# The normalised input of a two-layer trunk, 128 bytes further back in SBUF

## The chip, the cores and the metric

The kernel runs on one core of one Trainium2 chip. Its metric is the time of one execution on the device in microseconds, taken as the median of several; smaller is better.

## The reference, cut to what matters

Two layers, each made of an FFN, a token mixer and a second FFN. All three read a normalised and modulated input u, and add their gated result to the residual x (256 positions by 1024 channels). Everything is float32.

```python
for l in range(DEPTH):                       # 2
    mod = c_act @ w_ada[l] + b_ada[l]
    sh1, sc1, g1, sh2, sc2, g2, sh3, sc3, g3 = jnp.split(mod, 9, axis=-1)
    x = x + 0.5 * g1 * swiglu(modulate(x, sh1, sc1), ffn1_gate[l], ffn1_up[l], ffn1_down[l])
    x = x + g2 * token_mix(modulate(x, sh2, sc2), ..., w_in[l], ...)
    x = x + 0.5 * g3 * swiglu(modulate(x, sh3, sc3), ffn2_gate[l], ffn2_up[l], ffn2_down[l])
return rms_norm(x) * final_norm

def swiglu(u, w_gate, w_up, w_down):         # 1024 -> 2816 -> 1024
    return (jax.nn.silu(u @ w_gate) * (u @ w_up)) @ w_down
```

The token mixer projects u by w_in (1024 to 4024 columns), runs sparse attention and latent attention on the parts, merges them by sigmoid gates and projects the result by w_out.

## The kernel before

**Three matmuls for one.** Each product is made of float32r operands that are split in two parts: hi is the value rounded by ScalarE (L177 for weights, L336 for the input), lo is what is left, by VectorE (L182, L337). A product is hi x hi + hi x lo + lo x hi, so every tile of 128 x 128 takes three matmuls, all issued by the helper at L103. The weight's parts are whi and wlo, the input's uhi and ulo, the FFN's hidden layer's hh and hl.

**Which operand streams.** There are two forms. In `ws_tile` (L430) a weight tile of 128 columns is stationary and the input streams, 256 columns: the loop over groups of the gate and up projections (L606 to L622) and some parts of the token mixer (L701, L722, L881). In `xs_group` (L372) the input or the hidden layer is stationary and the weight streams, 512 columns (in the token mixer also 408, 288 and 256): the first 512 columns of gate and up, the merge gates, the down and the output projections. Each matmul loads its own stationary operand, also where it is the same as before.

**The order of the work.** Weights come by SP's DMA queue into four raw buffers. Scheduling within an engine follows the program's order, with a few exceptions that the change does not touch. Between the groups of an FFN the modulation of the next sub-layers is computed: VectorE sums the products (`ada_half`, L225), and TensorE then sums over partitions (the tiles `tr<-acc,ones` in the trace).

**Places in SBUF.** A pool lays its tiles one behind the other, in the order of their first use, and the pools lie one behind the other. The place of each tile in its partition follows from the sizes in front of it. In bytes, modulo 512 (the two halves of 128 positions and the eight channel blocks of the input are 512 and 1024 bytes apart, so the numbers hold for all of them):

| tiles | pool | modulo 512 |
|---|---|---|
| raw; whi and wlo (four in `wsp`, three in `fu`) | raws, wsp, fu | 96 |
| hh and hl (an FFN's hidden layer), cT (the latents), oa, ob, yt | ffn, tm | 96 |
| yk (half of the merged branches) | tm | 192 |
| x, uhi, ulo | keep | 288 |
| acc, g, and the scratch tiles xn, uf, rtmp | keep, scr | 288 |

The pool `keep` begins at 96. Its first tile is `apart` (L121), 48 floats or 192 bytes, that nothing reads; then come x (L123), uhi and ulo (L359, L360), then acc and g. `new_u` is called once for each sub-layer and hands out the same buffers each time.

Of the kernel before, what the change touches and what calls it, by code (L numbers as in the profile page):

```python
# [10 lines left out]
F32 = mybir.dt.float32  # L11
# [5 lines left out]
P = 128  # L17
# [60 lines left out]
def hybrid_trunk(ctx, tc, t, out):  # L78
    nc = tc.nc
# [7 lines left out]
    keep = ctx.enter_context(tc.tile_pool(name="keep", bufs=1))  # L87
# [30 lines left out]
    nc.gpsimd.memset(binit, 0.0)  # L118
    cact = const.tile([P, KD], F32, name="cact")
    nc.scalar.activation(cact, c_in, AF.Silu)  # L120
    apart = keep.tile([P, 48], F32, name="apart")  # L121
    nc.gpsimd.memset(apart, 0.0)
    x = keep.tile([P, NH, D], F32, name="x")  # L123
    colmask = tab[:, TAB_COL:TAB_COL + 32]
# [227 lines left out]
    def flush(ps):  # L352
        for p in list(ps):
            if p in pending:
                pending.remove(p)
                p[1]()

    def new_u():
        uhi = keep.tile([P, KD, S], F32R, name="uhi", tag="uhi")  # L359
        ulo = keep.tile([P, KD, S], F32R, name="ulo", tag="ulo")  # L360
        return uhi, ulo


# [743 lines left out]
    def start_norm(l, sub):  # L1107
        u = new_u()

        def post(hf):  # L1110
            pending.append([DELAY[hf], norm_mod(hf, u[0], u[1], mods[l, 3 * sub + 1], mods[l, 3 * sub])])
        return u, post
# [15 lines left out]
    fnorm = [None, None]  # L1128
    subs = [(l, sub) for l in range(DEPTH) for sub in range(3)]
    nxt = new_u()  # L1130
    xn = []
    for hf in range(NH):
# [60 lines left out]
```

## Time and profile before

| | |
|---|---|
| median of 3 runs | 1196.02 us (1194.01 to 1196.26) |
| the profiled execution | 1195.32 us |
| its span, from the first to the last instruction | 1193.5 us |
| TensorE busy, weight loads | 1156.5 us (97%), 1016.1 us (85%) |
| VectorE, ScalarE, POOL busy | 946.5, 640.8, 19.4 us |
| mean granted TensorE clock | 0.994 |

The ends of matmuls are modelled, so the time of one matmul in a row is not the pace: the pace is the distance between the starts of two that follow each other, or the length of an unbroken piece over its count. Several groups of the page are the same work for the three products.

### The profile page before, as it was taken

The numbers are of one execution on the slowest core, as the hardware profiler recorded it, in microseconds if no ns is written. First come the engines' busy times: TensorE is split into PE (matmuls) and PEld (weight loads), VectorE is DVE, ScalarE is ACT, GpSimd is POOL, SyncE is SP. The second block draws the span as 40 slices with busy tenths as digits, with TensorE's granted clock in tenths as the row PEclk, the third lists the DMA queues.
The fourth block names the chain that finished last, engine by engine and source line by source line (L and its number), as shares of the span: only waits on it lengthen the run. The fifth ranks groups of instructions, "written<-read, shape, count | busy, mean of one in ns | idle before, by whom it ended". The sixth has DMA issues, their size and how long they took to land.

```text
span 1193.5 us, 20212 instructions
## 1 busy us (share of the span) xinstructions
PE 1156.5 (97%) x7886; PEld 1016.1 (85%) x7886; DVE 946.5 (79%) x1885; ACT 640.8 (54%) x1152; POOL 19.4 (2%) x19
## 2 busy tenths in 40 slices
PE   5999999999999999999999999998999999999997
PEld 3799988799977789998879999787997778999985
DVE  4899998878888898798579889865878888865553
ACT  4444544557676565444455444454677756554441
POOL 0000000100000000000000000001000000000000
PEclk9999999899999999999999999999999999999999
DMA  9989999586623579989739979954664253985540
GB/s 330 318 292 327 343 344 326 200 237 197 177 74 107 177 231 306 308 290 321 271 106 317 319 261 364 342 191 139 181 194 118 78 188 131 298 260 201 173 146 36
DMA packets 201970, 274.95 MB, mean 230 GB/s; under 512 B 13613, under 2 KB 119815, under 8 KB 201875
## 3 DMA queue, kind: packets, MB, share of 16 engines
q1 hardware_dynamic: 201119, 273.02, 69.9%
q8 instruction: 62, 1.02, 0.3%
q10 hardware_dynamic: 756, 0.64, 0.2%
q14 instruction: 33, 0.27, 0.1%
HBM read 272.60 MB, written 1.05 MB: 229 GB/s over the span
## 4 chain that ended last, share of the span: by engine, by line
PE 87%; DVE 7%; DMA 2%; issue 2%; ACT 1%; SPq 1%; DVEq 0%; ACTq 0%
PE mm L103 78%; PE tr L106 3%; DVE wlo L182 3%; PE sc L103 2%; PE po L103 2%; DMA raw<-in_w_ada 2%; PE tr L103 2%; DVE win L710 1%; ACT whi L177 0%; DVE rs L305 0%; DVE rtmp L439 0%; DVE x L440 0%; DMA c_in<-in_c 0%; DVE kd L732 0%; DVE acc L528 0%
## 5 line engine op out<-in xcount | busy, mean ns | idle before, releaser
L182 DVE TENSOR_TENSOR wlo<-raw,whi 128x1024 fp32r<-128x1024 f32 (+5 forms) x400 | 428.0, 1085 | 122.6 <-ACT whi L177 121.4
L177 ACT ACTIVATE whi<-raw 128x1024 fp32r<-128x1024 f32 (+5 forms) x400 | 364.0, 935 | 235.6 <-PE mm L103 102.3
L103 PE MATMUL mm<-uhi,whi 128*128 128x256 f32 x1248 | 348.7, 279 | 0.0
L103 PE MATMUL mm<-uhi,wlo 128*128 128x256 f32 x1248 | 347.3, 278 | 0.0
L103 PE MATMUL mm<-ulo,whi 128*128 128x256 f32 x1248 | 347.3, 278 | 0.0
L103 PEld LDWEIGHTS mm<-ulo,whi 128*128 128x128 f32 x1248 | 236.4, 189 | 0.5
L103 PEld LDWEIGHTS mm<-uhi,whi 128*128 128x128 f32 x1248 | 234.3, 188 | 2.5 <-issue 1.8
L103 PEld LDWEIGHTS mm<-uhi,wlo 128*128 128x128 f32 x1248 | 234.4, 188 | 0.0
L225 DVE SCALAR_TENSOR_TENSOR acc<-raw,cact,acc 128x512 f32<-128x512 f32 x224 | 167.4, 749 | 6.3 <-DMA raw<-in_w_ada 3.4
L103 PE MATMUL mm<-whi,hh 128*128 128x512 f32 x352 | 138.3, 393 | 0.0
L103 PE MATMUL mm<-whi,hl 128*128 128x512 f32 x352 | 137.1, 390 | 0.0
L103 PE MATMUL mm<-wlo,hh 128*128 128x512 f32 x352 | 137.0, 389 | 0.0
L103 PE MATMUL mm<-wlo,uhi 128*128 128x512 f32 (+3 forms) x336 | 126.5, 377 | 3.7 <-DVE wlo L182 3.7
L103 PE MATMUL mm<-whi,uhi 128*128 128x512 f32 (+3 forms) x336 | 127.2, 381 | 2.6 <-ACT uhi L541 2.6
L103 PE MATMUL mm<-whi,ulo 128*128 128x512 f32 (+3 forms) x336 | 127.4, 380 | 1.7 <-DVE ulo L337 1.7
L482 ACT ACTIVATE hh<-hf 128x256 fp32r<-128x256 f32 x70 | 29.1, 416 | 95.7 <-DVE hf L481 95.7
L103 PEld LDWEIGHTS mm<-whi,hh 128*128 128x128 f32 x352 | 66.1, 188 | 15.1 <-issue 1.8
L103 PEld LDWEIGHTS mm<-whi,hl 128*128 128x128 f32 x352 | 66.1, 188 | 13.9
L103 PEld LDWEIGHTS mm<-wlo,hh 128*128 128x128 f32 x352 | 66.1, 188 | 13.4
L103 PEld LDWEIGHTS mm<-wlo,uhi 128*128 128x128 f32 x336 | 64.3, 191 | 14.1 <-DVE wlo L182 4.6
L103 PEld LDWEIGHTS mm<-whi,uhi 128*128 128x128 f32 x336 | 63.9, 191 | 13.7 <-ACT uhi L541 3.0
L103 PEld LDWEIGHTS mm<-whi,ulo 128*128 128x128 f32 x336 | 64.3, 191 | 12.5 <-DVE ulo L337 3.6
(243 smaller groups left out, 1347.5 us busy)
## 6 DMA issues: line engine op xcount, KB each, us to landing
raw<-in_w_ada SPq DMA_DIRECT2D x72, 1024.0 KB, 7.9
raw<-in_ffn_gate SPq DMA_DIRECT2D x41, 1024.0 KB, 7.5
raw<-in_ffn_up SPq DMA_DIRECT2D x41, 1024.0 KB, 6.2
raw<-in_ffn_down SPq DMA_DIRECT2D x40, 1024.0 KB, 7.4
raw<-in_w_in SPq DMA_DIRECT2D x18, 1024.0 KB, 6.5
raw<-in_w_in SPq DMA_DIRECT2D x16, 512.0 KB, 6.4
raw<-in_w_out SPq DMA_DIRECT2D x8, 1024.0 KB, 5.1
raw<-in_ffn_down SPq DMA_DIRECT2D x8, 512.0 KB
```

Source lines behind the costliest of these rows:

```text
L103: nc.tensor.matmul(o, a, b, start=start, stop=stop)
L106: nc.tensor.transpose(o, a, ident)
L177: nc.scalar.activation(a, s, AF.Copy)
L182: nc.vector.tensor_tensor(b, s, a.bitcast(F32), ALU.subtract)
L225: nc.vector.scalar_tensor_tensor(acc, rv[:, jj, :], cj, binit if j + jj == 0 else acc, ALU.mult, ALU.add)
L482: nc.scalar.activation(h[0][:, f, :], hf32, AF.Copy)
L710: nc.vector.tensor_tensor(win[i][jj * 64:(jj + 1) * 64, 8 * a:8 * a + 8, g, :], pv[g * 64:(g + 1) * 64, jj, :, a:a + 15], cols[0][jj * 64: ...
```

## The change

`apart` shrinks from 192 to 64 bytes, so x, uhi and ulo move back by 128 bytes, to 160 modulo 512. A new tile of 128 bytes, `behind`, is taken behind ulo, when `new_u` is called first, so acc, g and all later pools stay where they are. Nothing reads `behind`; it is set to zero once.

```diff
-    apart = keep.tile([P, 48], F32, name="apart")
+    apart = keep.tile([P, 16], F32, name="apart")
     nc.gpsimd.memset(apart, 0.0)
     x = keep.tile([P, NH, D], F32, name="x")
...
+    behind = []
+
     def new_u():
         uhi = keep.tile([P, KD, S], F32R, name="uhi", tag="uhi")
         ulo = keep.tile([P, KD, S], F32R, name="ulo", tag="ulo")
+        if not behind:
+            behind.append(keep.tile([P, 32], F32, name="behind"))
+            nc.gpsimd.memset(behind[0], 0.0)
         return uhi, ulo
```

With it the input lies 64 bytes past the place of the weights' parts, modulo 512, where it lay 192 past it. The order of instructions on TensorE, VectorE, ScalarE and SyncE stays as it was. On POOL one instruction comes in. Before, at the start of the program (apart, pad and binit are the tiles set to zero there, hid is one of the token mixer):

```order
L118 MEMSET binit 128x512
masks.py:199 ISA
masks.py:199 AFFINE_SELECT ident<-ident 128x128
L122 MEMSET apart 128x48
L129 MEMSET pad 128x80
L766 MEMSET hid 128x32
```

And now:

```order
L118 MEMSET binit 128x512
masks.py:199 ISA
masks.py:199 AFFINE_SELECT ident<-ident 128x128
L122 MEMSET apart 128x16
L129 MEMSET pad 128x80
L365 MEMSET behind 128x32
L771 MEMSET hid 128x32
```

One memset got shorter, and one of 32 floats a partition stands behind that of pad.

## Rows read from the trace of the kernel before

**Rows 1.** The page's busy times: us (share of the span) x instructions
```profile
PE 1156.5 (97%) x7886; PEld 1016.1 (85%) x7886; DVE 946.5 (79%) x1885; ACT 640.8 (54%) x1152; POOL 19.4 (2%) x19
```

**Rows 2.** The page's chain that ended last, by engine and line
```profile
PE 87%; DVE 7%; DMA 2%; issue 2%; ACT 1%; SPq 1%; DVEq 0%; ACTq 0%
PE mm L103 78%; PE tr L106 3%; DVE wlo L182 3%; PE sc L103 2%; PE po L103 2%; DMA raw<-in_w_ada 2%; PE tr L103 2%; DVE win L710 1%; ACT whi L177 0%; DVE rs L305 0%; DVE rtmp L439 0%; DVE x L440 0%; DMA c_in<-in_c 0%; DVE kd L732 0%; DVE acc L528 0%
```

**Rows 3.** The page's costliest groups: count | busy us, mean ns | idle before
```profile
L103 PE MATMUL mm<-uhi,whi 128*128 128x256 f32 x1248 | 348.7, 279 | 0.0
```

**Rows 4.** The chain in order of time: start us, length us, what
```profile
67.52 20.38 PE mm L103 x173
89.14 11.31 PE mm L103 x96
100.92 10.89 PE mm L103 x96
...
479.01 22.61 PE mm L103 x192
...
715.99 21.97 PE mm L103 x192
...
1057.94 127.72 PE mm L103 x840
```

**Rows 5.** Stretches, matmuls that read ulo: PE busy (count), clock, DMA share, GB/s
```profile
67.50:87.60 20.10, 15.98 (x58) 1.00 0.98 332
...
100.90:111.60 10.70, 8.72 (x32) 1.00 0.99 337
844.20:855.40 11.20, 8.96 (x33) 1.00 0.50 161
```

**Rows 6.** Weight loads from 480 to 500 us, then from 526 to 546
```profile
L103 PEld LDWEIGHTS mm<-ulo,whi 128*128 128x128 f32 x57 | 10.9, 192 | 0.0
...
L103 PEld LDWEIGHTS mm<-ulo,whi 128*128 128x128 f32 x59 | 11.1, 188 | 0.0
```

**Rows 7.** TensorE in order of time, cT streaming: start us, length us
```profile
293.85 0.40 PE L103 MATMUL mm<-cT,whi 128*128 128x256 f32 x2
...
294.93 0.28 PE L103 MATMUL mm<-cT,whi 128*128 128x256 f32 x1
```

**Rows 8.** The same, weights streaming in 256 columns, input stationary
```profile
277.77 0.28 PE L103 MATMUL mm<-whi,ulo 128*128 128x256 f32 x1
...
279.78 0.28 PE L103 MATMUL mm<-wlo,uhi 128*128 128x256 f32 x1
```

**Rows 9.** The same, 512 columns, hidden layer stationary
```profile
574.73 0.39 PE L103 MATMUL mm<-whi,hl 128*128 128x512 f32 x1
...
576.77 0.39 PE L103 MATMUL mm<-whi,hl 128*128 128x512 f32 x1
```

**Rows 10.** The same, 512 columns, input stationary
```profile
239.75 0.39 PE L103 MATMUL mm<-whi,uhi 128*128 128x512 f32 x1
...
241.81 0.39 PE L103 MATMUL mm<-whi,uhi 128*128 128x512 f32 x1
```

**Rows 11.** The same, 512 columns, yk stationary, and what follows it
```profile
405.90 2.97 PE L103 MATMUL mm<-us,yk 128*128 128x512 f32 x12
408.71 0.40 PE L103 MATMUL mm<-whi,yt 128*128 128x512 f32 x1
```

**Rows 12.** Groups by form: the 512-column matmuls with the input stationary
```profile
L103 PE MATMUL mm<-whi,ulo 128*128 128x512 f32 x240 | 97.8, 408 | 1.7 <-DVE ulo L337 1.7
```

**Rows 13.** Groups by form: VectorE's 512-column subtractions for ulo and wlo
```profile
L337 DVE TENSOR_TENSOR ulo<-uf,uhi 128x512 fp32r<-128x512 f32 x20 | 12.9, 688 | 1.0 <-ACT uhi L336 1.0
...
L182 DVE TENSOR_TENSOR wlo<-raw,whi 128x512 fp32r<-128x512 f32 x16 | 10.5, 685 | 0.4
```

**Rows 14.** POOL in order of time at the start: start us, length us
```profile
1.67 0.14 POOL L122 MEMSET apart<- 128x48 f32 x1
1.74 0.16 POOL L129 MEMSET pad<- 128x80 f32 x1
```

## The prediction, made before the change was run

> **What bounds the kernel now.** I read the page's busy table first: TensorE is busy for 1156.5 of 1193.5 us, VectorE for 946.5 [rows 1]. The chain that ended last says the same by itself: 87% of it is TensorE, 78% the matmuls of L103, and only 7% VectorE and 2% a DMA [rows 2]. So what counts is how fast matmuls follow each other, and the change touches no instruction of TensorE, only the address of one operand. The costliest groups name that operand: uhi with whi, 1248 matmuls of 256 columns, and two more groups of the same 1248 (ulo with whi, uhi with wlo) [rows 3], 3744 in all. In them the normalised input streams and a weight tile is stationary.
>
> Then I asked the chain in order of time, where each unbroken piece of matmuls has its length. The same 96 matmuls take 11.31 us at 89.14 and 10.89 us at 100.92; 192 take 22.61 us at 479.01 and 21.97 us at 715.99 [rows 4]. That is 117.8 ns a matmul in the first kind of piece (11310 / 96), 113.4 in the second (10890 / 96; in the 192 there is also one pause of 0.2 us at its entry). Each piece keeps its rate to its end: the last one holds 576 such matmuls and 264 of 512 columns; at 226.7 ns the 264 take 59.8 us, which leaves 67.9 us, 117.9 ns for each of the 576. TensorE is not idle in them and its granted clock is 1.00, the level of 2.4 GHz, in slow and fast pieces alike [rows 5]. So these are two patterns of the same work at the same clock. The only other thing that differs is the weight load under the matmul: of the slow pattern's three kinds one lasts 192 ns, against 188 in the fast one [rows 6]. I read this as the stationary operand's read and the streamed operand's read getting in each other's way, in a rhythm that keeps itself once it is there.
>
> **What the place has to do with it.** Places, all modulo 512: weights' parts 96, normalised input 288 (after: 160), cT 96, hidden h 96, yk 192. Four other groups show the same sizes at other distances.
> - 256 columns, distance 0 (cT streams, weights stationary): 293.85 to 294.93 is 9 matmuls in 1.08 us, 120 ns each [rows 7].
> - 256 columns, the roles turned (weights stream, input stationary, +192): 277.77 to 279.78 is 17 in 2.01 us, 118.2 [rows 8].
> - 512 columns, weights stream: hidden h stationary, distance 0, 9 in 2.04 us, 226.7 [rows 9]; normalised input stationary, +192, 9 in 2.06 us, 228.9 [rows 10]; yk stationary, +96, 12 in 2.81 us, 234.2 [rows 11].
> So the distance does count, by up to 7 ns in 120 and 8 in 227. The new distance, 64 (minus 64 where the input streams, plus 64 where it is stationary), is in no row; it has to be bounded.
>
> The Trainium skill says the opposite in "SBUF — State Buffer", section "Who interferes with whom": TensorE has two read ports of its own, one for the moving operand and one for the weight load, and "PE and ACT never wait on anyone". By that rule the operands' places would change nothing and the sum would stay at 1195.3. The trace does not bear it out: it has 113.4 and 117.8 for the same instruction, and 226.7, 228.9 and 234.2 for the same size. I keep the rule as the rival "no change", with a small chance.
>
> **The change part by part.** The profiled execution took 1195.32 us (span 1193.5 and 1.8 around it); the median of the runs shown is 1196.02, 0.7 above it, and I sum against the execution's own time.
>
> 1. The 3744 matmuls of 256 columns with the input streaming. Slow now: 173 + 4 x 96 + 2 x 192 + 576 on the chain [rows 4] and 96 at 844.2, which is not on it [rows 5]: 1613. Fast: 3744 - 1613 = 2131. Lower bound: the new distance lets every piece find the fast pattern, 1613 x 4.4 = 7.1 us less. Upper bound: it acts like its neighbour at distance 0, 120 ns for all, 2131 x 6.6 + 1613 x 2.2 = 17.6 us more. Which value? At both other distances that the trace shows for 256 columns the slow pattern holds nearly throughout [rows 7, 8]; a majority in the fast one is seen only at minus 192. And minus 64 lies nearer to 0 than to minus 192. I take four fifths in the slow pattern of 117.8, not the 120 of distance 0: 0.8 x 3744 = 2995 slow, 1382 more than now, x 4.4 = 6.1 us more. Nothing covers this: TensorE has no idle time there and is on the chain.
>
> 2. The matmuls of 512 columns with the input stationary, three groups of 240 [rows 12], 720. Bounds from the neighbours: 226.7 (distance 0) gives 720 x 2.2 = 1.6 us less, 234.2 (96) gives 720 x 5.3 = 3.8 us more. On the straight line between 0 and 96 the distance 64 stands at 231.7, 2.8 above now, 2.0 us; but 96 is the only one of these distances that is no multiple of 64, and the end at 0 is the safer one of the line, so I take 1.5 us more.
>
> 3. The 408-, 288- and 256-column projections with the input stationary, 3 x 96: a few ns each way at most as in step 2, within 0.9 us of nothing; taken as 0.
>
> 4. VectorE and ScalarE read and write x, uhi and ulo at the new place. VectorE's subtractions for ulo, at the old place, take 688 ns for 512 columns, and the split of a weight, all of whose operands lie at 96, takes 685 [rows 13]. So its rate does not see the place: 0, at most 3 ns x some 50, 0.2 us either way.
>
> 5. POOL: the memset of apart (138 ns at 1.67 us) becomes shorter and one like it is added behind that of pad, which starts at 1.74 us [rows 14]; POOL works for 19.4 us in the whole span [rows 1], so it has room. 0; were it not covered, 0.14 us. No queue of DMAs, no order on another engine and no wait is moved.
>
> Sum: 1195.3 + 6.1 + 1.5 = 1202.9, say 1203 us.
>
> **The rivals.**
> - It gets faster. The rhythm is set by where both reads meet, and 64 may be a distance at which they rarely do. For it: the fast pattern exists, is stable for hundreds of matmuls, and distance 0 gives a perfect 226.7 at 512 columns [rows 9]. Against: at 256 columns distance 0 is the worst of all [rows 7]. With four fifths of the 3744 in the fast pattern 749 stay slow, 864 x 4.4 = 3.8 us less, and half of step 2's gain, 0.8: 1190.7. With all of both it would be 1186.6, though around 67.5 to 87.6 us the DMAs already stand at 0.98 of their time [rows 5], so that the 0.8 us of that piece would become a wait for raw.
> - It falls back to distance 0's pattern, 120 ns for every matmul of 256 columns, from the first piece on: 17.6 us for step 1, and 1.5 for step 2: 1214.4. This is decided when the entry into each piece no longer finds either of the two patterns. For it: 64 is the nearest place to 0 and cT stays at 120 for whole runs [rows 7]. Against: a distance of 64 is not 0, and whether the pattern of 0 reaches that far no row shows.
> - No change, 1195.3. The places do not matter, or they repeat every 128 or 256 bytes, so that the new distance has the same mixture of pieces as now. For it: alike pieces last alike to the hundredth (four of 11.31 us, two of 22.61 [rows 4]), so the instructions before a piece, which the change leaves alone, may decide its pattern. Against: the four other distances, each with a rate of its own [rows 7 to 11]. The rule quoted above from the Trainium skill would give this case too.
>
> **How the numbers follow.** Forecast (some slow, 1198 to 1209): 0.43. Distance 0's pattern (over 1209): 0.13. Faster (below 1193): 0.26. No change: 0.18. A difference within 0.2%, 2.4 us, is what a measurement of this kernel can't tell from none. Faster 0.26, same 0.18, slower 0.56. Range: most of the faster case (1189 and up) and about half of the distance-0 case, so 1189 to 1212; the forecast's own range is 1198 to 1209. The median may stand 0.7 above the sum, which is within this.
>
> **What would show it.** Right: in the chain in order of time the pieces of 96 that now last 10.89 to 11.1 us last 11.3, those of 192 last 22.6, with weight loads of 192 ns in them; uhi pieces of 512 columns at 230 to 233. Wrong: pieces at 11.5 us (120 ns) and up, or the slow ones of now at 10.9. My reading itself would be wrong if no piece changed its rate, or if the time moved while they all kept theirs, through waits for raw, whi or wlo.

## The result, and the profile after

The changed kernel takes 1203.61 us, the median of four runs (1201.52 to 1207.09), against 1196.05 (four runs of before, 1194.01 to 1196.26): ratio 1.0071, 95% interval 1.0049 to 1.0093, 7.6 us slower. The profiled execution is the slowest of the four: 1207.09 us, span 1205.3. Of all runs below, one (1211.2 us in experiment 9, mean clock 0.988) was a slow one and is left out of its ratio.

The page's busy line and its costliest group of matmuls, as [rows 1, 3]:

```profile
PE 1168.5 (97%) x7886; PEld 1026.5 (85%) x7886; DVE 946.7 (79%) x1885; ACT 640.7 (53%) x1152; POOL 19.4 (2%) x20
...
L103 PE MATMUL mm<-uhi,whi 128*128 128x256 f32 x1248 | 350.3, 281 | 0.0
```

TensorE is busy for 12.0 us more, as much as the span has grown (11.8), and its weight loads, which overlap the matmuls, for 10.4 more. The busy times of VectorE, ScalarE and POOL are the same within 0.2 us.

The chain in order of time: start, length, what. These are the six pieces of [rows 4], and one of 177 that experiment 3 comes back to:

```profile
67.74 20.38 PE mm L103 x173
89.37 11.31 PE mm L103 x96
101.14 11.31 PE mm L103 x96
...
450.21 20.85 PE mm L103 x177
...
483.28 22.61 PE mm L103 x192
...
723.32 22.81 PE mm L103 x192
...
1069.74 127.72 PE mm L103 x840
```

The first two last what they did. The third had 10.89 us and has 11.31 now. The 192 at 723.32 had 21.97 and have 22.81. Slow pieces of before stayed as they were, within 0.01 us; every fast one became slow: 117.8 ns for each matmul (11.31 / 96; the 22.81 hold the pause of 0.2 us at their entry). The pattern of 113.4 ns is gone from the trace.

Stretches with the matmuls that read ulo, as [rows 5]: us, PE busy (count), loads busy, VectorE busy, clock, DMA share, GB/s.

```profile
67.70:87.80 20.10, 15.86 (x58) 10.66 (x57) 0.00 (x0) 1.00 0.99 330
101.10:112.00 10.90, 8.67 (x31) 5.77 (x32) 0.00 (x0) 1.00 0.97 330
```

The clock stands at 1.00 in the piece that turned slow, as in the one that was slow before.

Weight loads from 484 to 504 us, inside a slow piece, as [rows 6]:

```profile
L103 PEld LDWEIGHTS mm<-ulo,whi 128*128 128x128 f32 x58 | 10.9, 188 | 0.0
L103 PEld LDWEIGHTS mm<-uhi,whi 128*128 128x128 f32 x57 | 10.7, 188 | 0.0
L103 PEld LDWEIGHTS mm<-uhi,wlo 128*128 128x128 f32 x57 | 10.7, 187 | 0.0
```

All three kinds last 187 to 188 ns; the load of 192 ns that marked the slow pattern of before isn't there.

TensorE in order of time, 512 columns, the input stationary, as [rows 10]:

```profile
242.06 0.39 PE L103 MATMUL mm<-whi,ulo 128*128 128x512 f32 x1
...
246.26 0.39 PE L103 MATMUL mm<-whi,ulo 128*128 128x512 f32 x1
```

The second starts 18 matmuls behind the first: 4.20 us, 233.3 ns each, against the 228.9 of [rows 10].

The same view where cT streams, as [rows 7]:

```profile
297.04 0.40 PE L103 MATMUL mm<-cT,whi 128*128 128x256 f32 x2
...
298.84 0.40 PE L103 MATMUL mm<-cT,whi 128*128 128x256 f32 x2
```

Five such groups of three in 1.80 us: 120 ns, as before. cT and its weights kept their places.

VectorE's subtractions, as [rows 13], and POOL at the start, as [rows 14]:

```profile
L337 DVE TENSOR_TENSOR ulo<-uf,uhi 128x512 fp32r<-128x512 f32 x20 | 12.9, 685 | 1.1 <-ACT uhi L336 1.0
...
L182 DVE TENSOR_TENSOR wlo<-raw,whi 128x512 fp32r<-128x512 f32 x16 | 10.5, 684 | 0.3
```

```profile
1.72 0.16 POOL L129 MEMSET pad<- 128x80 f32 x1
1.82 0.12 POOL L365 MEMSET behind<- 128x32 f32 x1
```

685 and 684 ns, where 688 and 685 stood; the new memset takes 0.12 us behind that of pad.

One stretch belongs to this execution rather than to the change. Windows of after behind the second layer's first FFN (us, busy times of PE, loads, VectorE, ScalarE and POOL, then clock):

```profile
814.00:817.00 3.00, 1.18 (x5) 0.67 (x5) 3.00 (x2) 0.36 (x2) 3.00 (x2) 1.00 0.00 1
817.00:824.50 7.50, 6.15 (x20) 4.67 (x20) 6.85 (x12) 5.04 (x8) 1.69 (x1) 0.55 0.67 198
```

And before, over the same stage:

```profile
808.00:826.00 18.00, 15.84 (x72) 12.75 (x73) 13.06 (x19) 11.27 (x17) 2.50 (x1) 1.00 0.50 142
```

After 3 us in which TensorE was busy for 1.18, the granted clock fell: 0.55 of the full 2.4 GHz over the next 7.5 us, most of them at its lower level of 1.2. Before, it stood at 1.00 through that stage. The matched starts of after are 8.2 us behind those of before at 820.2 and 10.2 behind at 824.5, so the low clock cost 2.0 us. Of the four runs of after, this one had a mean clock of 0.989 and the others 0.995 to 0.997 and 1201.5 to 1203.7 us. This accounts for a part of what the profile's difference of 11.8 us stands above the 7.6 of the medians.

**Where the time went.** Starts of the same matmuls in both traces, matched one by one (a step is the distance from one start to the next): of the 3744 matmuls of 256 columns 3713 have an undisturbed step, and these take 437.32 us instead of 428.25, 9.1 more. Of the 720 of 512 columns with the input stationary, 616 have steps below 250 ns in both traces; they take 143.68 us instead of 141.75, 1.9 more (233.2 ns each instead of 230.1). Together 11.0 of the 11.8 us. With the 2.0 us of the low clock it would be 13.0; the other 1.2 come back, as a net sum, in pauses elsewhere.

### The profile page after: what moved, and what is told of

It is laid out like the page before. It is cut to its first block, busy times and chain, and to the rows that moved or that the text cites. A ratio compares the mean times of both kernels' runs of the same rounds, so it can differ in the third digit from the quotient of the medians.

```text
span 1205.3 us, 20213 instructions
## 1 busy us (share of the span) xinstructions
PE 1168.5 (97%) x7886; PEld 1026.5 (85%) x7886; DVE 946.7 (79%) x1885; ACT 640.7 (53%) x1152; POOL 19.4 (2%) x20
## 4 chain that ended last, share of the span: by engine, by line
PE 87%; DVE 7%; DMA 2%; issue 2%; ACT 1%; SPq 1%; DVEq 0%; ACTq 0%
PE mm L103 78%; PE tr L106 3%; DVE wlo L182 3%; PE sc L103 2%; PE po L103 2%; PE tr L103 2%; DMA raw<-in_w_ada 2%; DVE win L715 1%; ACT whi L177 0%; DVE rs L305 0%; DVE x L445 0%; DVE rtmp L444 0%; DMA c_in<-in_c 0%; DVE kd L737 0%; DVE acc L533 0%
## 5 line engine op out<-in xcount | busy, mean ns | idle before, releaser
L103 PEld LDWEIGHTS mm<-ulo,whi 128*128 128x128 f32 x1248 | 233.9, 187 | 0.5
```

The source lines that it names most:

```text
L103: nc.tensor.matmul(o, a, b, start=start, stop=stop)
```

## The experiments

"Distance" is the input's place less that of the weights' parts, in bytes modulo 512: 192 before, 64 after. Unless said otherwise acc and all pools behind it keep their places.

**1. Only x moved.** uhi and ulo stay at 288 (against the kernel before):

```diff
-    apart = keep.tile([P, 48], F32, name="apart")
+    apart = keep.tile([P, 16], F32, name="apart")
...
     x = keep.tile([P, NH, D], F32, name="x")
+    between = keep.tile([P, 32], F32, name="between")
+    nc.gpsimd.memset(between, 0.0)
```

> Only the residual x moves back to 160 modulo 512, uhi and ulo stay at 288. Theory A (the distance of the streamed and the stationary operand sets the matmuls' pattern): nothing of the 7.6 us is left, 1194 to 1197 us, the chain's pieces of 96 and 192 matmuls at 10.9 to 11.1 and 21.97 us again where they were before. Rival B (VectorE's and ScalarE's reads of x at the new place cost, and the matmuls only follow): about 1203 us.

Measured 1196.07 us, ratio 1.0004 (0.9985 to 1.0023). Its chain in order of time:

```profile
67.10 19.63 PE mm L103 x173
...
99.75 10.89 PE mm L103 x96
...
720.14 21.97 PE mm L103 x192
...
1062.02 127.72 PE mm L103 x840
```

The pieces of before, but for one: the 173 took 20.38 us [rows 4] and take 19.63 here, at 113.4 ns, although every tile that TensorE reads lies where it did. So the place of x, which only VectorE and ScalarE read, has no part in the 7.6 us; and a piece can change its pattern without a change of its operands' places.

**2. Everything moved by 128.** All behind the constants lies 128 bytes further on, and the distance stays 192:

```diff
-    pad(const, 320)
+    pad(const, 448)
```

> Everything behind the constants lies 128 bytes higher: input 416, weights 224, distance 192 as before. Theory A: as before, 1194 to 1197 us, the first piece of 96 matmuls after 100 us at 10.9 us. Rival C (the input's own place modulo 512 counts, not its distance from the weights): a time clearly off 1196, and pieces that all change.

Measured 1194.05 us, ratio 0.9985 (0.9963 to 1.0007): the input's own place does not count. Its chain:

```profile
667.44 21.77 PE mm L103 x192
...
1042.50 11.31 PE mm L103 x96
1054.28 125.16 PE mm L103 x840
```

The rates are those of before, 117.8 and 113.4. But other pieces have them: the 192 at 667.44 took 22.61 before, and the last piece took 127.72 [rows 4]. Experiments 9 and 10 follow that up.

**3 and 4. Distances 320 and 448**, which are 64 and 192 modulo 256 (against the changed kernel):

```diff
-    apart = keep.tile([P, 16], F32, name="apart")
+    apart = keep.tile([P, 80], F32, name="apart")     # e3; 112 in e4
...
-            behind.append(keep.tile([P, 32], F32, name="behind"))
+            behind.append(keep.tile([P, 96], F32, name="behind"))     # e3; 64 in e4
```

> The input at 416, distance 320, which is 64 modulo 256. Theory A with a period of 256 bytes: as the changed kernel, every piece of 96 at 11.31 us, the 512-column matmuls with the input stationary at 233.3 ns, 1201 to 1207 us. Theory A with a period of 512: another mixture; 320 is minus 192, the mirror of before, so the roles of the two forms swap: 256 columns as in the rows with weights streaming at +192 (118 ns nearly throughout, 1202 us and up).

> The input at 32, distance 448, which is 192 modulo 256 and minus 64 modulo 512. Theory A with a period of 256 bytes: as before, 1194 to 1197 us, with fast pieces of 10.9 us for 96. With a period of 512: minus 64, a mirror of the changed kernel; slow pieces throughout or a pattern of its own, 1200 us and up.

320: 1204.67 us, ratio 1.0073 (1.0042 to 1.0104). 448: 1195.34 us, 0.9995 (0.9979 to 1.0010). The chain of the one, then of the other:

```profile
100.87 11.31 PE mm L103 x96
...
451.59 20.07 PE mm L103 x177
...
677.35 22.61 PE mm L103 x192
```

```profile
87.62 10.90 PE mm L103 x96
98.99 11.31 PE mm L103 x96
...
667.00 22.61 PE mm L103 x192
...
712.87 21.97 PE mm L103 x192
```

448 has the pieces of before, those at 113.4 ns included, but for the first two of 96, of which now the first is fast and the second slow. With a period of 512 it should have taken 1200 us and up, so that theory falls. 320 alone would not have decided it, as both theories allow its time; its 512-column matmuls with the input stationary go at 233.2 ns, as after the change. It has the pieces of after but for one: the 177 that took 20.85 us there take 20.07, and the starts of 176 of them are 113.3 ns apart. So the distance modulo 256 is what counts, but at 64 the fast pattern is rare and not impossible: no piece in the trace of after has it, one in that of 320.

**5 to 8. Distances 0, 128, 160 and 224**, by the same two lines (`apart` left out or 32, 40, 56 floats; `behind` 48, 16, 8, 120).

> The normalised input's parts lie at 96 past a multiple of 512, as the weights' parts do: distance 0. Theory of the distance (what counts is how far the operand that streams lies from the stationary one, modulo 256): every matmul of 256 columns with the input's part streaming goes at the 120 ns that cT shows at distance 0 [rows 7], against 117.8 after the change and 113.4 or 117.8 before; over 3744 of them +17.6 us at most, less about 1.6 us as the 720 of 512 columns fall to 226.7 ns: 1208 to 1213 us. Rival, that distance 64 is a special case and 0 is clean (two parts of one place read side by side): 113.4 ns, about 1188 us.

> Input's parts at 224, distance 128. Two shapes of the theory of the distance. A slope with a sign (120 ns at 0, 117.8 at 64, some 115.6 at 192, so a fall of about 0.025 ns per byte up to 256): 116.7 ns per matmul of 256 columns, about 1200 us. A circle (what counts is the shorter way round, 128 is the farthest): all matmuls at 113.4 ns, about 1189 us. Rival of the first experiments, no theory of distance: 1196 us.

> Input's parts at 256, distance 160. Slope with a sign: 115.8 ns per matmul of 256 columns, about 1197 us. Circle (96 the shorter way): between 113.4 and the mixture of before, 1189 to 1195 us.

> Input's parts at 320, distance 224. Slope with a sign: 114.2 ns per matmul of 256 columns, about 1191 us, faster than before. Circle (32 the shorter way, nearer than 64): 118 to 120 ns, 1204 to 1213 us.

Measured: 1211.71 (1.0133, 1.0109 to 1.0157), 1207.86 (1.0108, 1.0085 to 1.0131), 1205.06 (1.0081, 1.0053 to 1.0109) and 1206.38 us (1.0094, 1.0069 to 1.0119). The chains of distance 0, 128, 160 and 224, in this order:

```profile
678.70 23.03 PE mm L103 x192
...
1072.83 129.00 PE mm L103 x840
```

```profile
66.25 20.76 PE mm L103 x173
...
678.50 22.78 PE mm L103 x192
...
1071.83 128.20 PE mm L103 x840
```

```profile
111.27 23.23 PE mm L103 x192
...
662.85 11.39 PE mm L103 x96
674.70 22.53 PE mm L103 x192
```

```profile
679.25 22.71 PE mm L103 x192
...
1070.86 128.02 PE mm L103 x840
```

Distance 0 came out as the theory said: 120 ns throughout. Both shapes for the others fell. 128 is no free place (118.7 ns, and in the first two long pieces 120.0), as the circle had it, and 224 isn't nearly free (118.3), as the slope had it. At 160 three patterns occur: 118.6 (11.39 / 96), 117.3 (22.53 / 192) and, in the 192 at 111.27, 120.0 between the starts behind the pause at its entry. None of the four has a piece at 113.4.

**9 and 10. Everything moved by 64 and by 192**, distance 192, as in the second (`pad(const, 384)` and `pad(const, 512)`). With this, acc, uhi and the rest move against the constants, ones and ident among them.

> Everything behind the constants lies 64 bytes further on; the input stays 192 past the weights, acc moves against ones, with which the sums between the groups are formed. Theory of the entry: at distance 192 a piece may run at 113.4 or at 117.8 ns, and the matmul before it decides which; pieces that follow the 512-column sums tr<-acc,ones change their pattern, the others keep theirs, no piece shows a third rate, and the time lies between 1189 (all fast) and 1203 us (all slow). Rival (the patterns of pieces have nothing to do with acc's place; what shift_all showed was chance): the same pieces slow as before, 1196 us.

> The same with 192 bytes. Theory of the entry: as above, with another choice of pieces behind the sums; only 113.4 and 117.8 ns, between 1189 and 1203 us. Rival: the same pieces as before, 1196 us.

By 64: 1193.32 us, ratio 0.9980 (0.9963 to 0.9997); by 192: 1193.41 us, 0.9983 (0.9959 to 1.0006). The chain of the shift by 64, then of that by 192:

```profile
464.39 10.90 PE mm L103 x96
475.76 21.77 PE mm L103 x192
...
1052.39 125.16 PE mm L103 x840
```

```profile
87.91 11.31 PE mm L103 x96
99.68 11.31 PE mm L103 x96
...
673.40 21.77 PE mm L103 x192
```

With 64, the eight pieces behind the sums all run at 113.4, 10.90, 21.77 and 125.16 us; before, one of the eight did, and the others had 11.31, 22.61 and 127.72. With 192 the six later ones do, and the two of 96 at the start are both slow, of which one was fast before [rows 4]. The slow piece of 96 at 844.2 [rows 5], which follows other matmuls, stays slow in both. No piece of 96 or more has a third rate. In the traces of before and of experiments 1 and 4, in which acc and ones keep their places, the six later pieces are all slow. So at distance 192 the entry decides, and for these pieces the places of what is read ahead of them belong to the entry. One part of the expectation failed: the piece of 173 ahead of the first sums changed too (20.38 us before; 171 steps of 113.5 ns in the shift by 64). It also changed in experiment 1, where nothing that TensorE reads had moved, so for this piece something else decides, and what that is stays open.

The profiled execution of the shift by 64 took 1187.19 us at a mean clock of 0.998, 8.1 less than that of before, 6.6 of it in the steps of the 256-column matmuls. The eight other runs in its ratio took 1190.4 to 1197.6 us at 0.990 to 0.997, so 2.4 us are left in the median. Its interval just excludes no change.

**11. Only ulo moved** to distance 64; uhi stays at 192 (against the kernel before):

```diff
         uhi = keep.tile([P, KD, S], F32R, name="uhi", tag="uhi")
+        if not between:
+            between.append(keep.tile([P, 96], F32, name="between"))
+            nc.gpsimd.memset(between[0], 0.0)
         ulo = keep.tile([P, KD, S], F32R, name="ulo", tag="ulo")
+        if not behind:
+            behind.append(keep.tile([P, 32], F32, name="behind"))
+            nc.gpsimd.memset(behind[0], 0.0)
```

> Only ulo moves to 160 (distance 64); x, uhi, acc and all else keep their distances. Theory of each by itself: a third of the matmuls of 256 columns (those with ulo) go as after the change and the rest as before: a third of 9.1 + 2.3 us, so about +3.8: 1200 us, pieces of 96 between 10.9 and 11.3. Theory of one rhythm for the piece (the three products alternate, and one that falls out of step holds them all): no piece at 113.4 ns any more, 1203 to 1206 us, as after the change.

Measured 1205.78 us, ratio 1.0081 (1.0058 to 1.0104). Its chain:

```profile
101.11 11.31 PE mm L103 x96
...
676.13 22.61 PE mm L103 x192
```

Every piece goes at 117.8 ns, as after the change, though only one matmul in three reads ulo. The three products of a piece share one rhythm. It isn't the rhythm of after, though: behind a matmul with ulo the next start follows after 119.0 ns on average, behind the two others after 117.0 and 117.3, where after has 117.6 to 117.9 for all three. The 512-column matmuls with the input stationary go at 231.6 ns, between the 230.1 of before and the 233.2 of after. (The place of ulo against uhi moves as well here; that this alone could do it is not excluded.)

**12. Distance 96**, again by the two lines (24 floats each).

> Input's parts at 192, distance 96, the same distance as yk's place has from the weights. So far distance 0 gave 120.0 ns per matmul of 256 columns, 64 gave 117.8, 128 gave 118.7, 160 gave 117.3 to 118.7, 224 gave 118.3, and only 192 has pieces at 113.4. Theory of the one free distance (192, and 192 modulo 256, is the only place at which the pattern without loss exists): 96 locks at one rate between 117 and 120 ns, no piece at 113.4, 1202 to 1212 us. Rival (a second free distance exists, and 96 with its odd step is it): pieces at 113.4, 1189 to 1196 us.

Measured 1212.10 us, ratio 1.0130 (1.0101 to 1.0158). Its chain:

```profile
678.22 23.04 PE mm L103 x192
...
1073.38 129.01 PE mm L103 x840
```

120 ns throughout, as at distance 0. Of the seven distances modulo 256 that were run, the fast pattern is common at 192 only; 64 has it in one piece (experiment 3), the other five in none.

No run moves the weights' parts alone. That it is the distance from them that counts, and not that from a third tile, is borne out by two pairs of rows: the input at distance 0 goes at 120 ns, as cT does there [rows 7], and here, at 96, the 512-column matmuls with the input stationary go at 234.0, where yk's at 96 have 234.2 [rows 11].

## Why the prediction was right

It was 1203.0 us, and the median is 1203.6. The mechanism was the right one: the same matmuls in the same order, paced by how far the streamed operand lies from the stationary one. Experiments 1 and 2 exclude x and the own place, 3 and 4 show it twice more, but for single pieces.

1. Matmuls of 256 columns, 6.1 us forecast: too small. Four fifths were to be slow, and in the trace all are (at 320, all but one piece of 177). The 2131 that went at 113.4 ns x 4.4 would be 9.4; the matched starts give 9.1. That they would stay at 117.8 and not go to distance 0's 120 was right. The reason given, "64 lies nearer to 0 than to 192", does not hold as a rule: 96 is farther from 0 and is at 120.
2. Matmuls of 512 columns, 1.5 us forecast: 1.9 in the 616 undisturbed steps; 2.3 if all 720 went so. The straight line between 0 and 96 gave 231.7 ns, and I took less than it; 233.3 was measured, nearly the 234.2 of yk's distance. Places are not on a line.
3. The projections of 408, 288 and 256 columns, forecast 0: the matched starts give 0.0.
4. VectorE and ScalarE, forecast 0: 685 against 688 ns, and experiment 1.
5. The memsets, forecast 0: covered, 0.12 us beside other work.

The sum of steps 1 and 2 is thus 3.4 us short against the profiled execution, and the forecast agrees with the median because the other runs of after are 3.4 to 5.6 us below the profiled one. The agreement to 0.6 us is partly luck. Of that distance 2.0 us are what the low clock cost the profiled execution; the others' mean clock was higher, 0.995 to 0.997 against 0.989. Where they save the rest I can't show, as only one execution of each kernel has a trace. That some of their pieces went fast, as one did at 320, is possible and not shown.

The rivals. "Faster" asked for a distance at which the reads rarely meet; by the time, 64 is none. "Distance 0's pattern" did not come at 64 but is just what distances 0 and 96 show, at 1211.7 and 1212.1 us (1214.4 was worked out). "No change" had a right half: places do repeat every 256 bytes, but 64 and 192 differ within these. The rule quoted from the Trainium skill ("SBUF — State Buffer", "Who interferes with whom"), by which no place could matter to TensorE, does not hold here: 1.0071 for one place against another, and 1.0133 at distance 0.

Of the markers, the lengths of the pieces were right (11.3 and 22.6 us), uhi's 512 columns came out at 233.3 where 230 to 233 stood. The weight load of 192 ns was wrong: in after's slow pieces all loads take 187 to 188, while at distance 0, in the last piece, all three kinds take 192. So it comes with some slow patterns and not with others; it was no sign of the collision, and my reading of it as the stationary operand's read being held up has lost its evidence. That the two operands' distance sets the pace is shown; which of the reads waits is not, and no run here takes one of them away.

## What to carry to other kernels

Where matmuls of 256 columns followed each other without a gap, the place of the streamed operand against the stationary one, modulo 256 bytes, was worth up to 6.6 ns in 120, here 1.3% of the kernel; look at the lengths of equal unbroken pieces in the chain, and if they come in two kinds, the places are among the first suspects, though a piece can change its kind without them (experiment 1). Try distances one by one rather than interpolate between them. Where two patterns are possible at one distance, shifting all tiles against what is read ahead of a piece may select the better one, as in experiment 9.

## What the runs showed of the hardware

**The rates are fractions of one step.** The piece of 192 behind the sums near 675 us takes 21.77 us without loss (experiments 2 and 10). Against that:

| distance modulo 256 | piece of 192, us | loss, us | loss over that of distance 0 | ratio of the time |
|---|---|---|---|---|
| 0 | 23.03 | 1.26 | 1 | 1.0133 |
| 96 | 23.04 | 1.27 | 1.01 | 1.0130 |
| 128 (two early pieces: 120.0 ns) | 22.78 | 1.01 | 0.80 | 1.0108 |
| 224 | 22.71 | 0.94 | 0.75 | 1.0094 |
| 64 (one piece at 320: 113.3 ns) | 22.61 | 0.84 | 0.67 | 1.0071, 1.0073 |
| 160 (other pieces: 118.6 and 120.0 ns) | 22.53 | 0.76 | 0.60 | 1.0081 |
| 192 | 21.77 or 22.61 | 0 or 0.84 | 0 or 0.67 | 0.9980 to 1.0004 |

The losses stand to each other as 1, 4/5, 3/4, 2/3, 3/5 and 0. With 1.26 us over 192 matmuls the full step is 6.6 ns. It would be easy to read this as matmuls that start either on time or one such step late. The starts in the traces do not bear that out. In the last piece of after the distances between them are 117, 118 and 119 ns (two are 116), and at distance 0 all are 120. At 96 six repeat (116, 123, 118, 121, 117 and 125), at 128 five (about 120, 115, 117, 122 and 120). So the means are fractions of one step, but the single starts are not shifted by whole steps; how the means come about stays open.

**Whether a choice of rates shows as spread** is open. Distance 96, with one rate in its trace, repeats closely (1211.67 to 1212.47 us in 4 runs), and before, with two, lies further apart (1192.8 to 1201.8 in the 59 runs beside the experiments). But distance 160, with three rates, keeps to 1204.06 to 1206.29, and after, with one, lies between 1201.5 and 1207.1. Whether the choice of pieces differs from run to run of one kernel, or only the clock, the traces cannot tell.
